# Attention results turned by transposes, two heads at a time, in halves of one PSUM bank

## The chip, the cores and the metric

The kernel runs on one core of a Trainium2 chip. The metric is the device time of one execution in microseconds; smaller is better. The engines are named as in the profile: PE (TensorE, matrix products), DVE (VectorE), ACT (ScalarE), POOL (GpSimd), and SP, which issues the DMAs.

## What is computed

Two layers over 2048 positions of width 1024. Each layer normalises x, projects it once, and gives the columns to four head groups of 256 columns each: A stick-breaking attention, B latent attention, C attention over the 256 best keys of each query, D differential attention. All results are gated, joined and projected back.

```python
def softmax_attention(q, k, v, scale):             # group B; C is the same over selected keys
    vis = chunk_visible(i, kk.shape[1])            # blocks of 128 queries, all keys up to the block
    s = einsum('bqhd,bshd->bhqs', qb, kk) * scale
    p = softmax(where(vis, s, -inf), axis=-1)
    return einsum('bhqs,bshd->bqhd', p, vv)

def diff_attention(...):                           # group D
    w = probs(q1b, k1b) - lam * probs(q2b, k2b)
    return einsum('bhqs,bshd->bqhd', w, vv)
y_d = rms_norm(od, diff_subln_g) * (1.0 - lam_init)
y = concatenate([silu(a_g) * y_a, silu(b_g) * y_b, silu(c_g) * y_c, silu(d_g) * y_d])
return x + einsum('bsn,nd->bsd', y, w_out)
```

## The kernel before

A layer is seven sweeps over 16 tiles of 128 queries, in the order a, h, d0, d1, b, c, o: group A with the scores of C's index, projections for later sweeps, the two halves of D, then B, C, and the output projection. For each tile of d0, d1, b and c there are units (two in d, four in b, two or four in c). A unit has a first part, which makes rows of probabilities (`att_row`: scores in PSUM, minimum and scaling on DVE, exponential with the sum on ACT, L847), and a second part, which multiplies them by the values (`att_pv`). The parts of neighbouring units, and projections of later tiles, are woven into each other by `merge` after costs that each part yields; the framework then orders the instructions of every engine by a timeline of its own, and each engine runs them in that order.

In `att_pv` the probabilities of up to four blocks of 128 keys are transposed on PE into a PSUM tile `tp` (L282), copied to SBUF by ACT (L284) or DVE (L286), and multiplied by the values (L866). The sums stand transposed in the PSUM tile `y`: even key blocks in partitions 0 to 63, odd ones in 64 to 127, and 128 columns for each head. `tp` has two buffers, `y` one, each a bank of 512 columns. In c and b one `y` holds four heads, in d two.

`att_out` finishes a tile. ACT copies `y` to SBUF (L875), and for each head PE multiplies that copy by `both`, two identity matrices of 64 above each other (L878). This adds even and odd blocks and turns the result, 128 queries by 64 columns. The product goes into `y` again. For b and c `norm_out` divides by the sums with one DVE product out of PSUM (L888) and writes 256 columns to `y` in DRAM (L889). In d two squares on ACT (L1093), the power -1/2 on POOL (`rstd`, L270 and L271), a small DVE product (L1095) and two larger ones (L1097) follow.

`y` serves other steps as well (`TG`): the transposes of queries and keys and the result of group A in sweep a (L354, L419, L431), and those of `prep_h` in sweep h (L1156). `o2` is the pool for what leaves, with two buffers. `psum` and `transposes` are helpers, so that most transposes have the line L282. The results wait in DRAM until sweep o reads them (L1302).

Of the kernel before, what the change touches and what calls it, by code (L numbers as in the profile page):

```python
# [10 lines left out]
F32 = mybir.dt.float32  # L11
# [29 lines left out]
EV = (0.6, 1.0, 0.6)  # L41
# [10 lines left out]
TG = {"ax": "pj", "at": "y", "ay": "y", "cp": "pj", "ct": "pj", "ao": "y", "kt": "pj", "dt": "pj", "ht": "y", "bt": "pj", "ot": "pj"}  # L52
# [55 lines left out]
class Trunk:  # L108
    def __init__(self, ctx, tc, I, out, layers=2):
        self.tc, self.nc, self.I, self.out, self.layers = tc, tc.nc, I, out, layers  # L110
        nc = self.nc
# [17 lines left out]
        ct = self.cst.tile  # L129
        ld = nc.sync.dma_start  # L130
# [3 lines left out]
        nc.scalar.copy(self.identr, self.ident)  # L134
        self.both = ct([128, 64], F32, name="both")
        ld(self.both, I["c_both"])
        self.identb = ct([128, 128], BF, name="identb")
# [20 lines left out]
        nc.vector.memset(self.chkC, float(TOPK))  # L158
        self.ev = 0


# [8 lines left out]
    def o2(self, shape, dtype=F32):  # L170

        return self.wk.tile(shape, dtype, name="o2", bufs=2)

# [5 lines left out]

    def psum(self, tag, shape=(128, 512)):  # L180
        return self.ps.tile(list(shape), F32, name=tag, bufs=PS[tag])

# [91 lines left out]
    def transposes(self, dst, srcs, eng="act", tag="pj"):  # L274

        nc = self.nc
        p = self.psum(tag, (128, 4, 128))
        m = srcs[0].shape[1]

        ident = self.identr if dst.dtype == F32R else self.ident  # L280
        for j, s in enumerate(srcs):
            nc.tensor.transpose(p[:m, j, :].bitcast(dst.dtype), s.bitcast(dst.dtype), ident)  # L282
        if eng == "act":
            nc.scalar.copy(dst, p[:m, :len(srcs), :])  # L284
        else:
            nc.vector.tensor_copy(dst, p[:m, :len(srcs), :])  # L286
# [402 lines left out]
    def ga_att(self, l, i, st):  # L689

        nc = self.nc
        yield 100.0
        t, v = st.pop(("a", i))
        o = i % 4 * 128
        nc.vector.tensor_copy(self.piece(st, "k", i, [128, 2, 512])[:, :, o:o + 128], t[:, 2:4])
        nc.vector.tensor_copy(self.piece(st, "v", i, [128, 4, 256])[:, i % 4, :], v)
        acc = self.o2([128, 2, 256])
        y = [self.psum("s", (128, 128)) for _ in range(2)]
        for b in range(i, -1, -1):
# [3 lines left out]
            for r in range(2):  # L703
# [3 lines left out]
                for p in range(2):  # L707
                    nc.tensor.matmul(z[r][:, p * 128:(p + 1) * 128], st["k"][b // 4][q, p, b % 4 * 128:b % 4 * 128 + 128], t[q, p, :],
                                     start=(b < i and p == 0), stop=True, skip_group_check=True)
# [14 lines left out]
            for p in range(2):  # L724
                for r in range(2):
                    hd = 2 * p + r
# [3 lines left out]
        ys = self.g2([128, 2, 128])  # L730
        for p in range(2):
            nc.vector.tensor_copy(ys[:, p], y[p])
        yo = self.g2([128, 2, 128])
# [135 lines left out]

    def att_out(self, i, y, nu):  # L870

        nc = self.nc
        h = 128 if i else 64
        ys = self.o2([128, 4, 128])
        nc.scalar.copy(ys[:h, :nu], y[:h].rearrange("p (a b) -> p a b", a=nu))  # L875
        p = self.psum(TG["ao"], (128, 4, 64))
        for u in range(nu):
            nc.tensor.matmul(p[:, u, :], ys[:h, u, :], self.both[:h], start=True, stop=True)  # L878
        return p[:, :nu]

    def norm_out(self, i, y, ls, col):

        nc = self.nc
        p = self.att_out(i, y, 4)
        rl = self.wk.tile([128, 4], F32, name="at_rl")
        nc.vector.reciprocal(rl, ls)
        yo = self.o2([128, 4, 64])
        nc.vector.tensor_mul(yo, p, rl[:, :, None].to_broadcast([128, 4, 64]))  # L888
        nc.sync.dma_start(self.y[i][:, col:col + 256].rearrange("p (a b) -> p a b", a=4), yo)  # L889

# [45 lines left out]
    def units_c(self, l, i, st):  # L936
        nb = i + 1
        ctx = {}
        m = 2 if i < PAIRED else 1
# [14 lines left out]
        def second(u):  # L954
            yield nb * m * 234.0 + 220.0
            if u == 0:
                ctx["y"] = self.psum("y")
            yield from self.att_pv(i, ctx[u], lambda j: st["cv"][j // 4][:, j % 4, :],
                                   ctx["y"][:, u * m * 128:(u + 1) * m * 128], EV[0])
            if u == 4 // m - 1:  # L960
                self.norm_out(i, ctx["y"], ctx["ls"], 512)
        return [(first(u), second(u)) for u in range(4 // m)]
# [82 lines left out]
    def units_d(self, l, i, st):  # L1045
# [32 lines left out]
        def second(u):  # L1078
# [6 lines left out]
            if u == 0:  # L1085
                return
            p = self.att_out(i, y[:, :256], 2)
            rl = wk.tile([128, 4], F32, name="at_rl")[:, :2]
            nc.vector.reciprocal(rl, ctx["l1"])
            yo = self.o2([128, 2, 64])  # L1090
            ss = wk.tile([128, 16], F32, name="ss")[:, :2]
            for h in range(2):
                nc.scalar.activation(yo[:, h], p[:, h], AF.Square, scale=rl[:, h:h + 1], accum_out=ss[:, h:h + 1])  # L1093
            rs = self.rstd("e", ss, 2, 64)
            nc.vector.tensor_mul(rs, rs, rl)  # L1095
            for h in range(2):
# [167 lines left out]
    def units_b(self, l, i, st):  # L1264
# [16 lines left out]
        def second(hd):  # L1281
            yield nb * 234.0 + 110.0
            if hd == 0:
                ctx["y"] = self.psum("y")
            yield from self.att_pv(i, [ctx[hd]], lambda j: st["bv"][j // 4][:, j % 4, hd * 64:(hd + 1) * 64],
                                   ctx["y"][:, hd * 128:(hd + 1) * 128], EV[2])
            if hd == 3:
                self.norm_out(i, ctx["y"], ctx["ls"], 256)
        return [(first(h), second(h)) for h in range(4)]
# [134 lines left out]
def consts():  # L1424
    import ml_dtypes
    r = np.arange(128)
    c = {}
    c["c_ident"] = np.eye(128, dtype=np.float32)
    c["c_both"] = np.tile(np.eye(64, dtype=np.float32), (2, 1))
    c["c_identb"] = np.eye(128, dtype=ml_dtypes.bfloat16)  # L1430
# [28 lines left out]
```

## Time and profile before

| | us |
|---|---|
| runs shown, median of 3 | 4232.53 (4230.74 to 4235.87) |
| profiled execution | 4232.69 |
| its span, first to last instruction | 4230.8 |
| mean granted clock of TensorE | 0.957 |

Busy time is the time in which an engine had an instruction at work. PE's instructions overlap, so a group's busy time is less than its count times its mean duration. A wait is the idle time of an engine before an instruction, put down to what released it.

### The profile page before, as it was taken

The page shows a single profiled execution, that of the slowest core. Times are in us where ns is not written, and L with a number is a line of the kernel's source. Part 1 is how long each engine was busy: PE and PEld are TensorE (multiplying, and loading weights), DVE is VectorE, ACT ScalarE, POOL GpSimd, SP SyncE. Part 2 cuts the span into 40 slices and gives each one's busy share as a digit, 9 for nine tenths or more (in the row PEclk, how much of TensorE's full clock was granted, in tenths as well). Part 3 has the DMA queues.
Part 4 walks back from the last instruction along what each step waited for, and adds up shares of the span by engine and source line. Part 5 has one row for each costly group of instructions (what it writes and reads, how often), then busy time and mean ns, then how long its engine had stood idle before and what let it go on. Part 6 is the DMA issues. An engine that isn't in the chain of part 4 may idle for free. (4 is left out here: it accounts for less than half of the span.)

```text
span 4230.8 us, 75339 instructions
## 1 busy us (share of the span) xinstructions
PE 3925.9 (93%) x25833; PEld 3246.6 (77%) x25833; DVE 2789.1 (66%) x10270; ACT 2318.9 (55%) x4790; POOL 1363.8 (32%) x2206
## 2 busy tenths in 40 slices
PE   6999997899988999999989999979899899999999
PEld 6887786778857777777878888768788577777787
DVE  3788677886876665563327897687868666555622
ACT  3566667565665554553125667666656555454621
POOL 2333212454554433210033332135444533232100
PEclk9999997999989999999999999979999799999999
DMA  3223552232210013214532236533232000132244
GB/s 125 100 94 124 180 183 86 83 85 89 86 37 26 18 38 100 79 46 142 164 109 102 100 117 212 159 94 93 77 96 82 27 20 19 48 102 69 68 134 138
DMA packets 227881, 396.49 MB, mean 94 GB/s; under 512 B 66336, under 2 KB 150432, under 8 KB 226976
## 3 DMA queue, kind: packets, MB, share of 16 engines
q1 hardware_dynamic: 227488, 391.59, 29.3%
q8 instruction: 206, 3.38, 0.3%
q14 instruction: 187, 1.53, 0.1%
HBM read 279.00 MB, written 112.49 MB: 93 GB/s over the span
## 5 line engine op out<-in xcount | busy, mean ns | idle before, releaser
L255 PE MATMUL pj<-w_hi,h_hi 128*128 128x384 f32 (+4 forms) x2560 | 872.6, 349 | 67.4 <-POOL w_hi L193 27.4
L256 PE MATMUL pj<-w_lo,h_hi 128*128 128x384 f32 (+4 forms) x2560 | 860.8, 344 | 9.9 <-POOL w_lo L187 6.3
L847 ACT ACTIVATE rw<-rw,at_mn 128x896 f32<-128x896 f32 (+15 forms) x512 | 615.8, 1204 | 171.6 <-DVE at_mn L846 151.6
L284 ACT COPY pt<-tp 128x512 f32<-128x512 f32 (+3 forms) x689 | 357.5, 529 | 431.3 <-PE tp L282 378.9
L255 PEld LDWEIGHTS pj<-w_hi,h_hi 128*128 128x128 f32 x2560 | 501.2, 196 | 104.8 <-POOL w_hi L193 31.0
L282 PE MATMUL tp<-ident,rw 128*128 128x128 f32 x3264 | 546.8, 289 | 36.6 <-DVE rw L1074 15.3
L259 PE MATMUL pj<-w_hi,h_lo 128*128 128x384 f32 (+4 forms) x2560 | 535.9, 339 | 0.0
L256 PEld LDWEIGHTS pj<-w_lo,h_hi 128*128 128x128 f32 x2560 | 501.2, 196 | 35.7 <-POOL w_lo L187 9.1
L282 PEld LDWEIGHTS tp<-ident,rw 128*128 128x128 f32 x3264 | 371.4, 145 | 174.0 <-issue 114.3
L843 DVE TENSOR_SCALAR_CACHE_REDUCE rw<-s 128x512 f32<-128x512 f32 x576 | 382.9, 685 | 125.2 <-PE s L837 80.2
L259 PEld LDWEIGHTS pj<-w_hi,h_lo 128*128 128x128 f32 x2560 | 439.2, 191 | 27.3 <-issue 11.5
L270 POOL TENSOR_SCALAR rs<-ss 128x2 f32<-128x2 f32 (+4 forms) x224 | 49.9, 223 | 1074.7 <-DVE ss L911 250.5
L538 ACT ACTIVATE junk<-sg,st_T 128x1152 int8<-128x1152 f32 (+4 forms) x224 | 293.8, 1311 | 75.3 <-DVE st_T L622 56.6
L271 POOL TENSOR_TENSOR rs<-rs,mhalf 128x8 f32<-128x8 f32 (+5 forms) x256 | 309.6, 1210 | 18.6
L286 DVE COPY pt<-tp 128x512 f32<-128x512 f32 (+3 forms) x247 | 153.2, 620 | 204.1 <-PE tp L282 164.9
L837 PE MATMUL s<-dk,qa 96*128 96x512 f32 (+3 forms) x640 | 235.0, 420 | 31.5 <-DVE rw L843 18.0
L837 PE MATMUL s<-bk,qa 128*128 128x512 f32 (+6 forms) x960 | 256.0, 391 | 2.2 <-DVE at_mn L841 1.6
L193 POOL TENSOR_SCALAR hl<-g 128x256 fp32r<-128x256 f32 (+1 forms) x384 | 143.8, 389 | 314.8 <-DVE g L452 60.1
L841 DVE CUSTOM_DVE_ANT_0 rw<-s,maskR 128x128 f32<-128x128 f32 (+3 forms) x400 | 187.7, 479 | 71.1 <-PE s L837 69.0
L187 POOL TENSOR_TENSOR hl<-g,hl 128x128 fp32r<-128x128 f32 (+1 forms) x384 | 215.7, 577 | 0.3
L866 PE MATMUL y<-pt,dv 128*64 128x128 f32 x2176 | 194.4, 305 | 19.8 <-DVE o L1097 12.4
L282 PE MATMUL pj<-identr,hl 128*128 128x128 f32 (+1 forms) x1280 | 172.9, 257 | 42.5 <-POOL hl L187 23.9
(267 smaller groups left out, 8256.2 us busy)
## 6 DMA issues: line engine op xcount, KB each, us to landing
h_hi<-hT SPq DMA_DIRECT2D x128, 512.0 KB, 3.8
h_lo<-hT SPq DMA_DIRECT2D x128, 512.0 KB, 4.9
x4a<-x SPq DMA_DIRECT2D x32, 512.0 KB, 4.8
hT<-h_hi SPq DMA_DIRECT2D x32, 512.0 KB, 2.7
hT<-h_lo SPq DMA_DIRECT2D x32, 512.0 KB, 3.4
x4a<-y SPq DMA_DIRECT2D x32, 512.0 KB, 3.5
x4b<-gate SPq DMA_DIRECT2D x32, 512.0 KB, 3.7
x4c<-x SPq DMA_DIRECT2D x32, 512.0 KB, 4.2
```

The source lines that it names most:

```text
L187: self.nc.gpsimd.tensor_sub(o, a, b)
L255: nc.tensor.matmul(p[:, :n], hi[:, k, :], whi[k], start=(k == 0), stop=False)
L256: nc.tensor.matmul(p[:, :n], hi[:, k, :], wlo[k], start=False, stop=False)
L259: nc.tensor.matmul(p[:, :n], lo[:, k, :], whi[k], start=False, stop=(k == kt - 1))
L271: nc.gpsimd.tensor_tensor(r, r, self.mhalf[:, :n], op=OP.pow)
L282: nc.tensor.transpose(p[:m, j, :].bitcast(dst.dtype), s.bitcast(dst.dtype), ident)
L284: nc.scalar.copy(dst, p[:m, :len(srcs), :])
L538: nc.scalar.activation(self.junk[:, :ns[g]], Sg[g], AF.Sign, bias=th[:, g:g + 1], scale=-1.0, accum_out=dst[:, g:g + 1])
L837: nc.tensor.matmul(p[:, :w], x, y, start=(k == 0), stop=(k == len(ops) - 1))
L843: nc.vector.tensor_scalar(o, p[:, :w], -scale, None, op0=OP.mult, op1=OP.min, accum_out=m)
L847: nc.scalar.activation(rw, rw, AF.Exp, bias=mn, scale=-1.0, accum_out=ls)
L866: nc.tensor.matmul(y[o:o + 64, :], v(j), pt[:, c * m:(c + 1) * m, :].rearrange("p a b -> p (a b)"), start=(j < 2), stop=(j >= nb - 2), ski ...
```

## The change

`y` becomes one tile that is made once, `halves`, two times 256 columns of one bank, and each call for `y` takes the other half. Transposes into `y` are done two at a time. `att_out` always takes two heads: ACT copies their sums to SBUF, PE transposes each head's block (128 by 128) into a buffer of `tp`, ACT copies both to SBUF, and POOL adds the columns of even and odd key blocks. `norm_out` is called for each pair of heads; its product by the reciprocal sums moves from DVE to POOL, and it writes 128 columns. In d the small product of `rs` and `rl` moves to POOL, and the squares and the last products read SBUF. `both` is gone, `o2` has four buffers, and an accumulator of the general path `ga_att`, which the profiled execution doesn't enter, takes its tile from another pool.

```diff
@@ -132,8 +132,6 @@
         ld(self.ident, I["c_ident"])
         self.identr = ct([128, 128], F32R, name="identr")
         nc.scalar.copy(self.identr, self.ident)
-        self.both = ct([128, 64], F32, name="both")
-        ld(self.both, I["c_both"])
         self.identb = ct([128, 128], BF, name="identb")
         ld(self.identb, I["c_identb"])
         self.maskA = ct([128, 256], BF, name="maskA")
@@ -157,6 +155,8 @@
         self.chkC = ct([128, layers, NT], F32, name="chkC")
         nc.vector.memset(self.chkC, float(TOPK))
         self.ev = 0
+        self.halves = self.ps.tile([128, 2, 256], F32, name="y", bufs=1)
+        self.nhalf = 0
 
 
     def g2(self, shape, dtype=F32):
@@ -169,7 +169,7 @@
 
     def o2(self, shape, dtype=F32):
 
-        return self.wk.tile(shape, dtype, name="o2", bufs=2)
+        return self.wk.tile(shape, dtype, name="o2", bufs=4)
 
     def x4(self, which, shape, dtype=F32):
         return self.wk.tile(shape, dtype, name="x4" + which, bufs=1)
@@ -178,6 +178,11 @@
         return self.wk.tile([128, 6, 128], F32R, name="qa", bufs=QA)
 
     def psum(self, tag, shape=(128, 512)):
+        if tag == "y":
+
+            self.nhalf ^= 1
+            y = self.halves[:, self.nhalf]
+            return y if len(shape) == 2 else y.rearrange("p (a b) -> p a b", b=shape[-1])
         return self.ps.tile(list(shape), F32, name=tag, bufs=PS[tag])
 
     def padd(self, o, a, b):
@@ -274,7 +279,11 @@
     def transposes(self, dst, srcs, eng="act", tag="pj"):
 
         nc = self.nc
-        p = self.psum(tag, (128, 4, 128))
+        if tag == "y" and len(srcs) > 2:
+            for j in range(0, len(srcs), 2):
+                self.transposes(dst[:, j:min(j + 2, len(srcs))], srcs[j:j + 2], eng, tag)
+            return
+        p = self.psum(tag, (128, 2 if tag == "y" else 4, 128))
         m = srcs[0].shape[1]
 
         ident = self.identr if dst.dtype == F32R else self.ident
@@ -867,26 +876,32 @@
                                  start=(j < 2), stop=(j >= nb - 2), skip_group_check=True)
             yield (109.0 + 125.0) * m * len(js)
 
-    def att_out(self, i, y, nu):
+    def att_out(self, i, y):
 
         nc = self.nc
         h = 128 if i else 64
-        ys = self.o2([128, 4, 128])
-        nc.scalar.copy(ys[:h, :nu], y[:h].rearrange("p (a b) -> p a b", a=nu))
-        p = self.psum(TG["ao"], (128, 4, 64))
-        for u in range(nu):
-            nc.tensor.matmul(p[:, u, :], ys[:h, u, :], self.both[:h], start=True, stop=True)
-        return p[:, :nu]
+        ys = self.o2([128, 2, 128])
+        nc.scalar.copy(ys[:h], y[:h].rearrange("p (a b) -> p a b", a=2))
+        p = self.psum("tp", (128, 4, 128))
+        for u in range(2):
+            nc.tensor.transpose(p[:, u, :h], ys[:h, u, :], self.ident[:h, :h])
+        po = self.o2([128, 2, 128])
+        nc.scalar.copy(po[:, :, :h], p[:, :2, :h])
+        if i == 0:
+            return po[:, :, :64]
+        yo = self.o2([128, 2, 64])
+        self.padd(yo, po[:, :, :64], po[:, :, 64:])
+        return yo
 
     def norm_out(self, i, y, ls, col):
 
         nc = self.nc
-        p = self.att_out(i, y, 4)
-        rl = self.wk.tile([128, 4], F32, name="at_rl")
+        rl = self.wk.tile([128, 2], F32, name="at_rl", bufs=4)
         nc.vector.reciprocal(rl, ls)
-        yo = self.o2([128, 4, 64])
-        nc.vector.tensor_mul(yo, p, rl[:, :, None].to_broadcast([128, 4, 64]))
-        nc.sync.dma_start(self.y[i][:, col:col + 256].rearrange("p (a b) -> p a b", a=4), yo)
+        p = self.att_out(i, y)
+        yo = self.o2([128, 2, 64])
+        self.pmul(yo, p, rl[:, :, None].to_broadcast([128, 2, 64]))
+        nc.sync.dma_start(self.y[i][:, col:col + 128].rearrange("p (a b) -> p a b", a=2), yo)
 
 
     def start_c(self, l, st):
@@ -953,12 +968,15 @@
 
         def second(u):
             yield nb * m * 234.0 + 220.0
-            if u == 0:
+            h = u * m
+            if h % 2 == 0:
                 ctx["y"] = self.psum("y")
+            o = h % 2 * 128
             yield from self.att_pv(i, ctx[u], lambda j: st["cv"][j // 4][:, j % 4, :],
-                                   ctx["y"][:, u * m * 128:(u + 1) * m * 128], EV[0])
-            if u == 4 // m - 1:
-                self.norm_out(i, ctx["y"], ctx["ls"], 512)
+                                   ctx["y"][:, o:o + m * 128], EV[0])
+            h += m
+            if h % 2 == 0:
+                self.norm_out(i, ctx["y"], ctx["ls"][:, h - 2:h], 512 + (h - 2) * 64)
         return [(first(u), second(u)) for u in range(4 // m)]
 
 
@@ -1084,15 +1102,15 @@
                                    y[:, u * 128:(u + 1) * 128], EV[1])
             if u == 0:
                 return
-            p = self.att_out(i, y[:, :256], 2)
-            rl = wk.tile([128, 4], F32, name="at_rl")[:, :2]
+            rl = wk.tile([128, 2], F32, name="at_rl", bufs=4)
             nc.vector.reciprocal(rl, ctx["l1"])
+            p = self.att_out(i, y)
             yo = self.o2([128, 2, 64])
             ss = wk.tile([128, 16], F32, name="ss")[:, :2]
             for h in range(2):
                 nc.scalar.activation(yo[:, h], p[:, h], AF.Square, scale=rl[:, h:h + 1], accum_out=ss[:, h:h + 1])
             rs = self.rstd("e", ss, 2, 64)
-            nc.vector.tensor_mul(rs, rs, rl)
+            self.pmul(rs, rs, rl)
             for h in range(2):
                 nc.vector.scalar_tensor_tensor(yo[:, h], p[:, h], rs[:, h:h + 1], gsub, op0=OP.mult, op1=OP.mult)
             o = 768 + 128 * st["half"]
@@ -1280,12 +1298,13 @@
 
         def second(hd):
             yield nb * 234.0 + 110.0
-            if hd == 0:
+            if hd % 2 == 0:
                 ctx["y"] = self.psum("y")
+            o = hd % 2 * 128
             yield from self.att_pv(i, [ctx[hd]], lambda j: st["bv"][j // 4][:, j % 4, hd * 64:(hd + 1) * 64],
-                                   ctx["y"][:, hd * 128:(hd + 1) * 128], EV[2])
-            if hd == 3:
-                self.norm_out(i, ctx["y"], ctx["ls"], 256)
+                                   ctx["y"][:, o:o + 128], EV[2])
+            if hd % 2 == 1:
+                self.norm_out(i, ctx["y"], ctx["ls"][:, hd - 1:hd + 1], 256 + (hd - 1) * 64)
         return [(first(h), second(h)) for h in range(4)]
```

## Rows read from the trace of the kernel before

**Rows 1.** The page's first part: busy time by engine

```profile
PE 3925.9 (93%) x25833; PEld 3246.6 (77%) x25833; DVE 2789.1 (66%) x10270; ACT 2318.9 (55%) x4790; POOL 1363.8 (32%) x2206
```

**Rows 2.** Stretches: us, busy us (x count) by engine, PEclk, DMA share, GB/s

```profile
0.00:436.00 436.00, 381.82 (x2361) 332.49 (x2362) 318.36 (x1163) 243.12 (x526) 141.01 (x195) 0.98 0.33 110
...
660.00:1268.00 608.00, 541.14 (x3876) 463.40 (x3875) 473.10 (x1784) 376.53 (x822) 284.34 (x466) 0.91 0.26 77
1268.00:1637.00 369.00, 353.59 (x2745) 281.16 (x2745) 224.66 (x774) 198.22 (x410) 135.33 (x250) 0.98 0.12 34
1637.00:1957.00 320.00, 310.21 (x2178) 233.97 (x2176) 178.07 (x563) 165.64 (x287) 72.78 (x116) 0.99 0.24 75
1957.00:2130.00 173.00, 171.26 (x795) 137.56 (x795) 57.20 (x89) 33.20 (x58) 8.51 (x10) 1.00 0.55 181
```

**Rows 3.** PE's groups: busy us, mean ns | idle before, releasers

```profile
L282 PE MATMUL tp<-ident,rw 128*128 128x128 f32 x3264 | 546.8, 289 | 36.6 <-DVE rw L1074 15.3 <-ACT pt L284 10.8 <-DVE pt L286 3.5
...
L878 PE MATMUL y<-both,o 128*128 128x64 f32 (+1 forms) x768 | 106.1, 275 | 1.2 <-ACT o L875 1.0
```

**Rows 4.** A hand-off in sweep c, in order of time: start, us

```profile
3873.84 1.09 PE L282 MATMUL tp<-ident,rw 128*128 128x128 f32 x8
...
3874.89 1.10 PE L878 MATMUL y<-both,o 128*128 128x64 f32 x8
...
3875.83 1.05 PE L282 MATMUL tp<-ident,rw 128*128 128x128 f32 x8
...
3876.03 0.42 DVE L888 TENSOR_TENSOR o<-y,at_rl 128x256 f32<-128x256 f32 x1 [0.35 <-PE y L878]
...
3876.81 1.52 PE L866 MATMUL y<-pt,cv 128*64 128x256 f32 x12
```

**Rows 5.** What PE waited for: us in total, times, longest us

```profile
PE pj L282 <- POOL hl L187: 23.9, 19, 3.2
...
PE y L866 <- DVE o L1097: 16.9, 9, 4.8
...
PE tp L282 <- ACT pt L284: 10.8, 13, 3.6
...
PE y L878 <- ACT o L875: 1.0, 3, 0.5
```

**Rows 6.** The end of one tile of sweep d, in order of time

```profile
2998.01 0.37 ACT L875 COPY o<-y 128x256 f32<-128x256 f32 x1 [0.83 <-PE y L866]
...
2998.44 0.66 PE L878 MATMUL y<-both,o 128*128 128x64 f32 x4
...
3003.74 0.19 POOL L270 TENSOR_SCALAR rs<-ss 128x2 f32<-128x2 f32 x1
...
3006.73 0.47 DVE L1097 SCALAR_TENSOR_TENSOR o<-y,rs,gsub 128x64 f32<-128x64 f32 x2
```

**Rows 7.** ACT's groups, shapes kept apart

```profile
L875 ACT COPY o<-y 128x512 f32<-128x512 f32 x60 | 35.2, 586 | 38.0 <-PE y L866 37.8
...
L875 ACT COPY o<-y 128x256 f32<-128x256 f32 x60 | 22.1, 368 | 36.8 <-PE y L866 36.5
...
L284 ACT COPY qa<-y 128x512 f32<-128x512 f32 x32 | 18.8, 588 | 5.3 <-PE y L282 5.3
```

**Rows 8.** GpSimd's groups, shapes kept apart

```profile
L190 POOL TENSOR_TENSOR tab<-ci_cs,gain 128x128 f32<-128x128 f32 x64 | 31.5, 512 | 2.7 <-DMA ci_cs<-c_rope 2.0 <-DVE g L1042 0.6
...
L184 POOL TENSOR_TENSOR rw<-rw 128x128 f32<-128x128 f32 x40 | 21.2, 530 | 2.9
...
L187 POOL TENSOR_TENSOR qb<-g,qb 128x32 fp32r<-128x32 f32 x32 | 8.6, 268 | 0.0
```

**Rows 9.** DVE's groups, shapes kept apart

```profile
L1074 DVE SCALAR_TENSOR_TENSOR rw<-rw,d_c 128x512 f32<-128x512 f32 x192 | 163.8, 890 | 2.1
...
L1311 DVE TENSOR_TENSOR x4a<-x4a,x4b 128x512 f32<-128x512 f32 x64 | 41.5, 686 | 33.1 <-DMA x4a<-y 15.6 <-ACT x4b L1307 11.7 <-ACT h_hi L1315 5.8
```

More of the change, by code (lines that the diff above doesn't have):

```diff
@@ L696, in ga_att @@
         nc.vector.tensor_copy(self.piece(st, "v", i, [128, 4, 256])[:, i % 4, :], v)
-        acc = self.o2([128, 2, 256])
+        acc = self.pt([128, 2, 256])
         y = [self.psum("s", (128, 128)) for _ in range(2)]
@@ L1428, in consts @@
     c["c_ident"] = np.eye(128, dtype=np.float32)
-    c["c_both"] = np.tile(np.eye(64, dtype=np.float32), (2, 1))
     c["c_identb"] = np.eye(128, dtype=ml_dtypes.bfloat16)
```

## The prediction

> **What bounds the kernel now.** I read the page's first part, then a table of busy time by stretch, then PE's groups and waits, and last two places in the order of time. TensorE (PE) is busy for 3925.9 of 4230.8 us, and GpSimd (POOL) for a third [rows 1]. The stretches show that this is not one limit: sweep b (1268 to 1637 us) and sweep c (1637 to 1957) have PE busy for 354 of 369 and 310 of 320 us at a granted clock of 0.98 and 0.99, so that there PE's work is the time. Sweeps d0 and d1 (660 to 1268) have PE busy for 541 of 608 at 0.91, with DVE at 473: a mixture of PE's work and of waits on DVE, POOL and ACT [rows 2]. The second layer repeats these sweeps.
>
> **PE's work.** For each head, `att_out` multiplies the saved result by `both` (L878): 4 heads in 64 calls (b, c) and 2 heads in 64 calls (d) make 384 products, in the trace 768 instructions, 106.1 us of busy time [rows 3]. The change puts 384 transposes of a 128x128 float32 block in their place. That operation is in the trace: the transposes of probabilities (L282 into `tp`) are one instruction each, 3264 for 546.8 us, or 0.168 us each [rows 3]. So 384 x 0.168 = 64.3 us stand for 106.1, a saving of 41.8 us. The order of time says the same: eight L878 start at 3874.89 and what follows them at 3875.83, 0.94 us for four heads; eight transposes start at 3873.84 and L878 follows at 3874.89, 1.05 us, or 0.52 for four [rows 4]. 0.94 - 0.52 = 0.42 for four heads, times 96 such sets, is 40 us.
>
> By count 256 of the 384 are in b and c, where PE is the limit: 27.9 us, counted in full. The other 128 are in d: 13.9 us, counted at PE's busy share there, 541/608, so 12.4. Together -40.3. Fewer instructions also mean fewer weight loads, and I give nothing for that.
>
> **The hold of `y`.** Before, `y` is one PSUM buffer which serves the sums, and then the product of L878; it comes free only when the last reader of that product is done. In d that is a long way round: copy by ACT at 2998.01, L878 at 2998.44, squares on ACT, the power on POOL (its first step at 3003.74), L1097 ending at 3007.20. That is 9.2 us [rows 6]. PE stood for it 9 times, 16.9 us in all [rows 5]. After it, the copy alone (0.37 us, [rows 6]) ends the hold, since the product goes into `tp` and is copied on to SBUF. What is late next at these places is the following unit's own probabilities, so I take half: -8; bounds 0 and -16.9.
>
> In b and c `y` now changes hands after two heads, 128 times instead of 64, and GpSimd's share comes behind. PE's list of waits has no entry for L888, the reader which released `y` there [rows 5]: at the one shown, `y` is free at 3876.45 and PE is in transposes until 3876.81 [rows 4]. The new hand-off needs ACT's copy only. The next sums must in any case wait for their own first transposes and these for an eviction, so I put it at 0. If that cover is gone the price is the copy, 0.37 us each; that is the slow rival below.
>
> **`tp`.** The two transposes take one of two slots until ACT has copied them out, so the next unit's second set of transposes waits for copy, transposes and copy. An ordinary eviction has the same length, and waits for evictions by ACT cost PE 10.8 us over all sweeps [rows 5]. The transposes themselves stand at the head of PE's queue until the copy of `y` is done: L878 paid 1.0 us in 128 calls for this [rows 5], 192 calls pay 1.5.
>
> **ACT.** 192 copies of 256 columns at 0.368 replace the copies of 512 (35.2 us) and 256 (22.1) [rows 7], and 192 more at the same price bring the transposes to SBUF: 141 for some 61 (the few small ones included), +80. In sweeps a and h each set of transposes into `y` becomes two (2+2 and 2+1), which costs ACT 2 x 0.37 - 0.59 = 0.15 for each of the 32 in a [rows 7] and about as much in h, +10 in all. ACT goes from 55% to 57%. What waits behind a copy are exponentials and evictions; bounds 0 to 192 x 0.37 = 71 if PE stood for each second copy. I take +4 with the 1.5 above in it, near the bottom, because so little of PE's waiting is for ACT now.
>
> In a and h the second pair may have to wait until the first is copied, if the two halves are kept apart as one bank: 64 x 0.37 = 24 at most, 0 where other work covers it, and -1 or so if the halves run freely. Sweep a has PE busy for 382 of 436 us [rows 2], which leaves other causes of idle time as cover: +4.
>
> **GpSimd and DVE.** Added on POOL are 192 additions and 128 products of 128 elements, for which the nearest rows give 0.51 and 0.53 us, and 64 products of 2 elements at 0.27 or less [rows 8]: 320 x 0.52 + 64 x 0.27 = 184 us, 32% to 37%. These results are needed sweeps later, or by a late step of d, so they do not hold PE. But the splits of projections queue behind them on POOL, and PE waits for those: 23.9 us for L187 [rows 5]. The load of POOL in d and b rises by a tenth to a quarter, so between 0 and as much again; I take +6. DVE loses L888 and L1095, some 40 us less the extra reciprocals, mostly off PE's path: 0. The y transfers in b and c double in number and halve in size; they wait on SP for POOL instead of DVE, and loads behind them may start later. I put that inside the +6.
>
> There is a reason in the trace against moving work to POOL. L1074, which reads two SBUF tensors, takes 890 ns for 512 columns in sweep d, where POOL is 47% busy; L1311, also with two SBUF inputs of that width, takes 686 in sweep o, where POOL is 5% busy [rows 2, 9]. The difference of 0.2 us on 192 instructions is 39 us of DVE; POOL's added tenth in d would add 4, and I leave it in the range. The Trainium skill, page "GPSIMD Engine Reference", section "Key points", names this: GpSimd shares its SBUF interfaces with VectorE and contends with DVE instructions that have two SBUF inputs. The two rows agree with it, though the operations differ.
>
> **Sum.** -40.3 - 8 + 4 + 4 + 6 = -34.3. The profiled execution took 4232.7 (span 4230.8 and 1.9 around it), 0.2 over the median, so 4198 on the median's scale. With ACT's bound of 71 left to the slow rival, the bounds of the other terms run from -41.8 - 16.9 = -58.7 (4174) to -40.3 + 4 + 24 + 24 = +11.7 (4244).
>
> **Rivals.** *Each hand-off is exposed (slower).* The halves lie in one bank. If a write into one half is ordered after the read of the other, alternating buys no overlap, and PE stands for ACT's copy each time. Price: 128 hand-offs in b and c and 64 in a and h, 192 x 0.37 = 71 us, so 4198 + 71 - 4 = 4265. It decides from 34/192 = 0.18 us exposed for each. Against it: b and c keep PE fed at 96% through hand-offs of 1.5 us (3874.89 to 3876.45) [rows 2, 4]. For it: they come twice as often. The Trainium skill, page "PSUM — Partial Sum Buffer", section "PSUM bank collisions raise a hardware error", says that guards should go by bank and quadrant, not by address; that is this rival's condition, and no row of before shows two halves in use. Chance 0.18.
>
> *The relief is spent elsewhere (same).* d ends on DVE, and PE's saving in d and at `y` turns into waits for L1074 and its like, while POOL's queue and the copies take as much as b and c give: 27.9 against 24 (POOL's whole bound) gives 4228. It needs POOL's waits to double. Chance 0.17.
>
> *More comes back (faster).* d's clock of 0.91 between the two levels 1.2 and 2.4 GHz means 18% of 608 us at the lower, 219 us over both layers. If the 16.9 us of waits go wholly, and with them an eighth of d's 134 us of PE idle time, and low stretches shrink in proportion, 27 us at half speed return 14. Together -41.8 - 16.9 - 14 + 14 = -59, or 4174; with POOL's and ACT's costs at nothing 4160. Chance 0.13.
>
> **Numbers.** The forecast holds 0.52, most of it within 25 us of its value. Faster by over 0.2% (8.5 us, about what a measurement tells from no change): 0.52 and 0.13, and a little of the same case, 0.67; same 0.15; slower 0.18. The range goes from 4160 to 4250, which leaves out half of the slow rival and the tails.
>
> **What would show it.** In the profile after: no L878, 384 more transposes into `tp` at 0.17 us of busy time; PE's busy time down by 40; the wait of `y` for DVE gone in d; waits of `y` for ACT below 0.18 us per hand-off; POOL up by 184 us, ACT by 90; b and c shorter by some 13 us in each layer, d by 10. I am wrong if b and c do not get shorter, or if PE's idle time grows by more than 35 us.

## The result

The changed kernel takes 4299.56 us (median of 5, 4297.81 to 4304.52), beside 4232.58 of the kernel before: ratio 1.0153 (95% interval 1.014 to 1.0167), 67 us slower. The forecast was 4198. The profiled execution took 4304.5, its span is 4302.7 us, 71.9 longer, at nearly the same mean clock (0.956); it is the slowest of the five.

PE's busy time was to fall by 40 us. The page of the changed kernel shows it risen by 25.9 instead, and the span by more than that, so PE's idle time rose too, from 304.9 to 350.9 us. ACT rose by 77 and GpSimd by 153:

```profile
PE 3951.8 (92%) x25449; PEld 3200.4 (74%) x25449; DVE 2768.1 (64%) x10206; ACT 2395.9 (56%) x5108; POOL 1517.0 (35%) x2578
```

Line numbers have moved: the products with the values, L866 before, are L875 now; ACT's copy of `y`, L875 before, is L884, and the new copy of the transposed result L889; the evictions of `tp` (its copies to SBUF), L284 and L286, are L293 and L295. Four words are used below. A *hand-off* is the passing of `y` from the sums of one pair of heads (before, of one tile) to the next. The *block* is the two transposes that turn a pair of heads (in the kernel before, the products by `both` in their place), a *set* the up to four transposes that share a buffer of `tp`, and a *run* of products a row of them with no other PE instruction between.

PE's groups of the changed kernel (busy us, mean ns | idle before) have two lines to set against [rows 3]. The block's transposes (L887; a smaller form for the first tiles brings them to 384 and 78.2 us) are 27.9 us cheaper than the 768 products. The same 3264 transposes of probabilities (now L291) cost 15.1 us more than before:

```profile
L291 PE MATMUL tp<-ident,rw 128*128 128x128 f32 x3264 | 561.9, 291 | 49.6 <-DVE rw L1092 25.0 <-ACT o L889 9.8 <-POOL rw L189 5.5
...
L887 PE MATMUL tp<-ident,o 128*128 128x128 f32 x360 | 73.4, 286 | 12.1 <-ACT o L884 11.5
```

PE's waits in the changed kernel (us in total, times, longest), against [rows 5]: the 16.9 us for L1097 are gone, the head of the block's transposes waits 20.6 us for ACT's copy of `y` where L878 waited 1.0, and the products wait 40.3 us (24.4 and 15.9) for evictions of `tp`:

```profile
PE pj L291 <- POOL hl L192: 34.1, 29, 7.8
...
PE y L875 <- ACT pt L293: 24.4, 38, 2.5
PE tp L887 <- ACT o L884: 20.6, 27, 4.5
...
PE y L875 <- DVE pt L295: 15.9, 25, 1.4
...
PE tp L291 <- ACT o L889: 9.8, 11, 3.4
```

Before, the products' wait for evictions was 15.4 us:

```profile
PE y L866 <- DVE pt L286: 8.5, 13, 1.4
...
PE y L866 <- ACT pt L284: 6.9, 9, 2.8
```

So the wait at the block itself grew by 19.6 us, and the products' wait for evictions by 24.9.

Where in the kernel: the lengths of the sweeps, each counted from the start of the last result's DMA of one sweep to that of the next, both layers added (us; the last two columns are experiments described below).

| sweep | before | after | e1_y_half | e13_y_whole |
|---|---|---|---|---|
| a | 935.8 | 953.7 | 950.5 | 940.8 |
| h | 302.1 | 308.4 | 310.3 | 301.0 |
| d0 and d1 | 1262.8 | 1254.9 | 1246.9 | 1259.0 |
| b | 731.2 | 759.8 | 730.4 | 729.7 |
| c | 671.5 | 710.8 | 638.9 | 637.5 |
| o | 317.4 | 306.4 | 315.2 | 317.5 |

Sweeps b and c, where the prediction counted its surest gain, are 68 us longer, nearly the whole loss; the others change by -11 to +18 and together by 5. The four stretches b, c, b, c of the changed kernel (us, then PE, PEld, DVE, ACT and POOL busy, clock, DMA share, GB/s) show PE idle for 25.5, 23.0, 25.6 and 15.2 us; before, cut in the same way, it was 14.3, 10.2, 11.6 and 8.4. Of the 68 us, 45 are idle time of PE and 23 are busy time. The clock stays at 0.96 to 0.99, near the upper of its two levels:

```profile
1261.60:1639.80 378.20, 352.68 (x2658) 274.83 (x2658) 218.69 (x781) 207.29 (x456) 163.71 (x310) 0.97 0.12 35
1639.80:1994.50 354.70, 331.65 (x2166) 236.10 (x2167) 176.86 (x556) 178.17 (x333) 102.45 (x177) 0.97 0.23 72
3412.90:3794.50 381.60, 355.99 (x2663) 276.90 (x2661) 219.11 (x781) 211.06 (x461) 164.82 (x316) 0.96 0.12 35
3794.50:4150.60 356.10, 340.86 (x2247) 246.45 (x2248) 177.64 (x563) 182.69 (x337) 95.02 (x167) 0.99 0.25 78
```

PE's instructions in the order of time show what has changed. One hand-off in sweep c of the changed kernel (start, us, count, idle before):

```profile
3955.49 0.65 PE L875 MATMUL y<-pt,cv 128*64 128x256 f32 x4
3956.07 0.72 PE L846 MATMUL s<-ck,qa 128*128 128x512 f32 x2
3956.63 0.51 PE L264 MATMUL pj<-w_hi,h_lo 128*128 128x384 f32 x2
3956.98 0.38 PE L887 MATMUL tp<-ident,o 128*128 128x128 f32 x2
3957.20 0.60 PE L291 MATMUL tp<-ident,rw 128*128 128x128 f32 x4
3958.05 0.66 PE L291 MATMUL tp<-ident,rw 128*128 128x128 f32 x4 [0.25 <-ACT o L889]
3958.63 0.65 PE L875 MATMUL y<-pt,cv 128*64 128x256 f32 x4
3959.22 0.66 PE L291 MATMUL tp<-ident,rw 128*128 128x128 f32 x4
3960.04 0.65 PE L875 MATMUL y<-pt,cv 128*64 128x256 f32 x4 [0.17 <-DVE pt L295]
3960.62 0.66 PE L291 MATMUL tp<-ident,rw 128*128 128x128 f32 x4
```

Before, eight transposes of the next unit ran ahead of L878 and more behind it, and the products then came twelve at a time [rows 4]. Here no transpose of the next unit stands between the last products (3955.49) and the block (3956.98); scores and a piece of a projection fill the time there. The next unit begins behind the block, its second set waits for the copy of the block (0.25 us), and PE then goes to and fro, four transposes and four products. That no transpose stands ahead of the block is so throughout. By the starts of PE's instructions, the mean number of transposes of probabilities between a pair's last product and its block was 4.2 in b and 5.3 in c before; after the change it is 0 in every one of the 192 hand-offs.

A part of the rise of PE's busy time comes with it. The profile models where a PE instruction ends, so these are times from a start to the next start, idle time left out. A product that another product follows takes 0.067 us on the mean and the last of a run 0.23; a transpose of probabilities that another follows takes 0.13, the last ahead of a product 0.22 to 0.23. The kernel before has 700 runs of products, the changed one 810, and `e1_y_half` below 697; the changed kernel has 122 more such last transposes than `e1_y_half`. By these means that is 113 x 0.16 + 122 x 0.10, some 30 us more for the same work, about half of the 63.5 us by which the busy times of the two differ. The other half was not traced to a cause.

### The profile page after: what moved, and what is told of

It reads as the page before. It is cut to its first block, busy times and chain, and to the rows that moved or that the text cites. A ratio compares the mean times of both kernels' runs of the same rounds, so it can differ in the third digit from the quotient of the medians.

```text
span 4302.7 us, 75444 instructions
## 1 busy us (share of the span) xinstructions
PE 3951.8 (92%) x25449; PEld 3200.4 (74%) x25449; DVE 2768.1 (64%) x10206; ACT 2395.9 (56%) x5108; POOL 1517.0 (35%) x2578
## 4 chain that ended last, share of the span: by engine, by line
PE 60%; DVE 17%; ACT 8%; POOL 5%; issue 5%; DMA 5%; SPq 0%; ACTq 0%; POOLq 0%; DVEq 0%
PE y L875 9%; PE s L846 8%; PE pj L260 8%; PE tp L291 8%; PE pj L261 7%; PE pj L264 7%; PE s L260 3%; PE s L261 3%; PE s L264 3%; DVE sc L515 2%; ACT junk L547 2%; DMA w_raw<-w_in 2%; PE pj L291 2%; ACT rw L856 2%; DVE rw L850 1%
## 5 line engine op out<-in xcount | busy, mean ns | idle before, releaser
L260 PE MATMUL pj<-w_hi,h_hi 128*128 128x384 f32 (+4 forms) x2560 | 877.5, 351 | 70.9 <-POOL w_hi L198 25.9
L291 PE MATMUL tp<-ident,rw 128*128 128x128 f32 x3264 | 561.9, 291 | 49.6 <-DVE rw L1092 25.0
L293 ACT COPY pt<-tp 128x512 f32<-128x512 f32 (+3 forms) x689 | 359.4, 529 | 408.5 <-PE tp L291 390.8
L264 PE MATMUL pj<-w_hi,h_lo 128*128 128x384 f32 (+4 forms) x2560 | 524.1, 339 | 0.0
L291 PEld LDWEIGHTS tp<-ident,rw 128*128 128x128 f32 x3264 | 373.2, 145 | 188.4 <-issue 116.7
L295 DVE COPY pt<-tp 128x512 f32<-128x512 f32 (+3 forms) x247 | 153.1, 620 | 272.6 <-PE tp L291 255.3
L189 POOL TENSOR_TENSOR o<-o 128x128 f32<-128x128 f32 x180 | 89.9, 499 | 508.7 <-ACT o L889 457.6
L291 PE MATMUL pj<-identr,hl 128*128 128x128 f32 (+1 forms) x1280 | 174.7, 258 | 51.6 <-POOL hl L192 34.1
L514 ACT ACTIVATE pt<-s 128x512 f32<-128x512 f32 (+3 forms) x304 | 158.3, 547 | 109.0 <-DVE sc L515 60.7
```

The source lines that it names most:

```text
L260: nc.tensor.matmul(p[:, :n], hi[:, k, :], whi[k], start=(k == 0), stop=False)
L264: nc.tensor.matmul(p[:, :n], lo[:, k, :], whi[k], start=False, stop=(k == kt - 1))
```

## The experiments

Times are medians; a ratio is to the kernel before on the same chip, with its 95% interval.

| run | us | ratio |
|---|---|---|
| e1_y_half | 4205.34 | 0.9932 (0.991 to 0.9953) |
| e7_before_tp | 4279.09 | 1.0121 (1.01 to 1.0142) |
| e2_dve | 4294.55 | 1.014 (1.0123 to 1.0157) |
| e3_whole | 4294.45 | 1.0134 (1.0117 to 1.0151) |
| e5_both | 4225.76 | 0.9985 (0.9974 to 0.9997) |
| e4_four | 4202.51 | 0.9931 (0.9911 to 0.995) |
| e6_defer | 4303.82 | 1.0172 (1.0153 to 1.0191) |
| e10_split | 4266.10 | 1.01 (1.008 to 1.012) |
| e12_dummy_y | 4231.16 | 1.001 (0.9999 to 1.002) |
| e11_dummy_tp | 4285.60 | 1.0135 (1.0115 to 1.0155) |
| e14_dummy_free | 4209.58 | 0.9951 (0.9935 to 0.9968) |
| e15_dummy_late | 4250.49 | 1.0045 (1.0028 to 1.0062) |
| e9_y_dve | 4222.90 | 0.9975 (0.9963 to 0.9987) |
| e13_y_whole | 4194.63 | 0.9922 (0.9902 to 0.9942) |

**The block's place.** The changed kernel with one line other:

```diff
-        p = self.psum("tp", (128, 4, 128))
+        p = self.psum("y", (128, 2, 128))
         for u in range(2):
             nc.tensor.transpose(p[:, u, :h], ys[:h, u, :], self.ident[:h, :h])
```

> The changed kernel (4299.6 us) with one edit: the two transposes of att_out go into the other half of y instead of a buffer of tp. Theory tp (the result's block takes one of the two tp buffers for a round trip over ACT, so the next unit's transposes of probabilities can't run ahead): most of the loss comes back, 4200 to 4245 us, and ACT's and POOL's added work stays. Theory ACT (two copies per pair stand in ACT's queue in front of evictions and exponentials): unchanged, 4285 to 4315. Theory POOL and theory splits (a, h): unchanged as well.

The place alone is worth 94 us, and without it the change is a gain. PE's page line and a hand-off of this kernel in sweep c:

```profile
PE 3888.3 (93%) x25449; PEld 3203.2 (76%) x25449; DVE 2769.0 (66%) x10206; ACT 2391.1 (57%) x5110; POOL 1516.7 (36%) x2578
...
3850.80 1.08 PE L875 MATMUL y<-pt,cv 128*64 128x256 f32 x8
3851.82 0.76 PE L291 MATMUL tp<-ident,rw 128*128 128x128 f32 x5
3852.42 0.44 PE L887 MATMUL y<-ident,o 128*128 128x128 f32 x2
3852.91 0.66 PE L291 MATMUL tp<-ident,rw 128*128 128x128 f32 x4
3853.49 1.08 PE L875 MATMUL y<-pt,cv 128*64 128x256 f32 x8
3854.51 0.66 PE L291 MATMUL tp<-ident,rw 128*128 128x128 f32 x4
```

Five transposes stand ahead of the block again (4.6 on the mean in b, 5.3 in c), and the next products are eight in a row: 1.02 us from start to start, where the changed kernel takes 0.59 for four. PE's busy time is 63.5 us below the changed kernel's for the same instructions, with 697 runs of products.

The reverse, on the kernel before: its product by `both` goes into `tp`.

```diff
-  "ao": "y"
+  "ao": "tp"
```

> The kernel before (4232.6 us) with one edit: the product by both goes into a buffer of tp instead of y. Both theories of tp: slower, by the 95 us that the block's place made in the changed kernel for 192 blocks, times 128/192, so 4275 to 4310; in the trace no transpose of probabilities stands between the last sums and L878. Theory that the loss needs the second ACT copy as well (here DVE frees the block at once): 4232 to 4250.

47 us for 128 blocks, with no transposed block, no second copy, no halves and no new work on GpSimd: 0.37 us each, against 0.49 for the 192 above. Here too no transpose stands between last product and block, in all 128.

**GpSimd, and the splits of sweeps a and h.** The change with additions and products back on DVE:

```diff
-        self.padd(yo, po[:, :, :64], po[:, :, 64:])
+        nc.vector.tensor_add(yo, po[:, :, :64], po[:, :, 64:])
...
-        self.pmul(yo, p, rl...)
+        nc.vector.tensor_mul(yo, p, rl...)
```

> The changed kernel with the additions and both products on DVE instead of POOL. Theory POOL (splits of projections queue behind the new work and PE waits for them): 4230 to 4260. Theories tp and ACT: within 12 us of the changed kernel, 4288 to 4312, as DVE has a third of its time free.

The change with the transposes of three and four in a and h whole:

```diff
-            for j in range(0, len(srcs), 2):
-                self.transposes(dst[:, j:min(j + 2, len(srcs))], srcs[j:j + 2], eng, tag)
-            return
+            p = self.halves.rearrange("p a (b c) -> p (a b) c", c=128)
...
```

> The changed kernel, but sets of three and four transposes in sweeps a and h go into the whole bank at once, with one copy, as before the change. Theory splits (the second pair waits for the first pair's copy): sweeps a and h return to 611 and 614 us per layer from 635 and 627, 4260 to 4275 in all. Theories tp, ACT and POOL: within 12 us of the changed kernel.

Each gives back 5 us of 67, and its interval overlaps that of the change; neither is the cause. In `e3_whole` sweeps a and h are as short as before (1238.6 us together, 1237.9 before, 1262.1 after the change; the kernel before has 630 and 608 by layer in this cut, not the expectation's 611 and 614), but later sweeps give most of that back.

**Halves and hand-offs of two heads alone.** The change, but with the product by `both` into the other half and DVE reading it there:

```diff
-        p = self.psum("tp", (128, 4, 128))
-            nc.tensor.transpose(p[:, u, :h], ys[:h, u, :], self.ident[:h, :h])
+        p = self.psum("y", (128, 2, 128))
+            nc.tensor.matmul(p[:, u, :64], ys[:h, u, :], self.both[:h], start=True, stop=True)
...
+        return p[:, :, :64]
```

> Halves and hand-offs of two heads as in the changed kernel, but the result is turned by the product with both into the other half of y, and DVE takes it from PSUM; no second ACT copy, no block in tp, no POOL work. It isolates the halves and the doubled hand-offs with PE's old work. Theory tp: 4225 to 4250. Theory ACT: half of the loss stays, 4255 to 4280, since 192 copies of y instead of 128 remain. Theory hand-off (twice as many turns of y in b and c by themselves): 4280 or more.

At 0.9985 nothing is lost by twice as many hand-offs and the split sets of a and h together. PE's saving without the halves is measured on the kernel before with the transposes of all its heads in `y`, one copy by ACT, and the rest on GpSimd:

```diff
-        p = self.psum(TG["ao"], (128, 4, 64))
-            nc.tensor.matmul(p[:, u, :], ys[:h, u, :], self.both[:h], start=True, stop=True)
+        p = self.psum("y", (128, 4, 128))
+            nc.tensor.transpose(p[:, u, :h], ys[:h, u, :], self.ident[:h, :h])
+        po = self.o2([128, 4, 128])
+        nc.scalar.copy(po[:, :nu, :h], p[:, :nu, :h])
...
```

> The kernel before with the transposes alone: four heads (two in d) in the whole bank of y, one ACT copy out of it, addition and product on POOL; no halves, no block in tp. PE's cheaper work by itself, 4232.6 - 40 and some 6 back for POOL and ACT: 4190 to 4210. If the halves are what pays in the variant with the block in y (4205), this stays at 4220 or above, since y is held for one more ACT copy.

It gives 29 us, as much as `e1_y_half` (0.9931 and 0.9932): the halves add nothing that can be told. It is not PE's cheaper work alone, since DVE's product goes to GpSimd here too, and `e9_y_dve` below shows that this counts.

**Why the place costs.** First the block was written later, behind the next unit's first two sets of transposes, together with the copy of `y`:

```diff
             if self.ev >= 1:
                 self.ev -= 1
+            if j0 == step or nb <= step:
+                self.flush()          # att_out and what follows of the unit before
...
```

> The changed kernel with its block still in tp, but att_out of a pair is written behind the next unit's first two sets of transposes (first one, where a unit has one). Two theories of why the block in tp costs so much. Order: buffers of tp are given out in the order of the program, so no transpose of the next unit can pass the block, and PE has nothing between the last sums and the block; then the later place brings most back, 4205 to 4240 us. Occupancy: one of two buffers is gone for ACT's round trip wherever it is taken; then 4275 or more.

No gain, and not conclusive, since the copy of `y`, for which the block waits, went back with it: `tp` waited 44.3 us for that copy. So the copy stayed in its place and the block alone was moved:

```diff
+                y = self.att_save(i, ctx["y"])          # the copy to SBUF, at once
-                self.norm_out(i, ctx["y"], ...)
+                self.late = lambda: self.norm_out(i, y, ...)
```

> The change with the block in tp as it is, but written later: the copy of y to SBUF stays where it was, and the two transposes of the block, their copy and what follows are written behind the next unit's first two sets of transposes. Theory order (the buffers of tp are handed out in the written order, and the block holds back the next unit's transposes because it has to wait for the last product and the copy of y): by the time the block's turn comes its copy is long done, so most of the 94 us that the block's place cost comes back, 4205 to 4240 us. Rival occupancy (the block costs because it takes one of two buffers from first transpose to the end of ACT's copy, some 0.8 to 1 us, whenever it comes): 4270 to 4305, as the change. Between: both have a share.

It gives back 22 of the 94 us (1.0100 against 1.0153). Theory order wanted most of it back, and as stated it fails here; 4266 lies just below the rival's range, where the expectation gives both a share. To part the wait from the hold, one transpose that nobody reads was added to `e1_y_half`. It goes into `tp`, or as a control into `y`:

```diff
+        t = self.psum("tp", (128, 4, 128))                                # e11
+        nc.tensor.transpose(t[:, 0, :h], ys[:h, 0, :], self.ident[:h, :h])
...
+        nc.tensor.transpose(p[:, 0, :h], ys[:h, 0, :], self.ident[:h, :h])  # e12, p is in y
```

> The variant with the block in the other half of y (4205 us), and beside it one transpose of the copied y into a buffer of tp that nobody reads: it takes a buffer for one transpose, 0.15 us, and needs no copy by ACT, but it stands in the written order between the units. Work added on PE: 192 transposes of 0.168, at most 32 us. Theory order: the next unit's transposes can't pass it, so the time is well above its control (the same transpose into y): control plus 50 us or more, 4270 to 4310. Rival occupancy: a buffer held for 0.15 us costs little, control plus 0 to 15.

> The control of the dummy in tp: the same added transpose of the copied y, but into the half of y that the block's own transposes overwrite at once. Both theories: the added work alone, 0 to 32 us above 4205, so 4205 to 4238.

The same transpose costs 54 us more in `tp` than in `y`, though no copy holds its buffer. In `e11_dummy_tp` no transpose of probabilities stands between last product and block in any of the 192, and there are 809 runs of products; in `e12_dummy_y` they are 4.8 (b) and 5.4 (c), with 706 runs. The control itself is 33 us (0.0078) above `e1_y_half`, the full price of its 192 transposes. Then the wait was taken away with the taker left in its place (the transpose is of a constant), and the taker moved behind the next unit's two sets:

```diff
-        nc.tensor.transpose(t[:, 0, :h], ys[:h, 0, :], self.ident[:h, :h])
+        nc.tensor.transpose(t[:, 0, :h], self.ident[:h, :], self.ident[:h, :h])   # e14
...
+            ys, h = self.late                                   # e15, in flush, as in e6
+            nc.tensor.transpose(t[:, 0, :h], ys[:h, 0, :], self.ident[:h, :h])
```

> The variant with the block in the other half of y, and one transpose into a buffer of tp that nobody reads, at the same place in the written order, but of a constant (the identity), so that it has no copy to wait for. Its two relatives: the same transpose of the copied y into y took 1.001 of before, into tp 1.0135. Theory wait (the next unit's transposes stand behind a taker of tp that has to wait for the last product and ACT's copy of y): without that wait the time is near the first, 1.000 to 1.004 of before, 4226 to 4245. Rival turn (a third taker in the order of the two buffers costs by itself, since it ties each set of transposes to the one before it): near the second, 1.010 to 1.015, 4270 to 4295.

> The variant with the block in the other half of y, and the unread transpose of the copied y into tp, written behind the next unit's first two sets of transposes. Theory wait: the copy is done by then and nobody reads the buffer, so near the control, 1.000 to 1.005 of before, 4226 to 4250; what the deferred block itself still lost (1.010) is then ACT's copy out of tp, for which a buffer stays taken. Rival turn: a taker of tp at any place costs, 1.008 to 1.014, 4262 to 4290.

Without the wait the extra taker costs nothing that can be told from `e1_y_half` (0.9951 against 0.9932, intervals overlapping), although it is 192 more transposes for PE, and 5.5 (b) and 6.0 (c) transposes pass ahead of the block. That is below both ranges of the expectation, on the side of theory wait. Moved behind two sets it costs 15 us over the control (1.0045 against 1.0010), inside the range of theory wait. The added transposes in PE's groups, of `e11_dummy_tp` and then of `e14_dummy_free`, show the difference in what they wait for:

```profile
L887 PE MATMUL tp<-ident,o 128*128 128x128 f32 x180 | 52.9, 294 | 12.7 <-ACT o L884 12.1
```

```profile
L887 PE MATMUL tp<-ident 128*128 128x128 f32 x180 | 58.0, 322 | 3.2 <-ACT pt L293 2.4 <-DVE pt L295 0.3
```

So the wait is shown: a taker of `tp` that waits for the last product and for ACT's copy of `y` keeps back every later transpose into `tp`. It is worth 54 us against the control in `y`, and 78 us (0.0184) against `e14_dummy_free`. The rest of the 94, 40 or 16 us by subtraction, was not parted by a run of its own. Three things point to the hold, the buffer being taken until ACT has copied the block: the little that `e10_split` gives back, `e15_dummy_late`, whose late taker is not copied and which is 23 us (0.0055) faster than `e10_split`, and the 0.25 us in the hand-off above. But when a block is written elsewhere the whole order of PE changes with it (`e10_split` has 881 runs of products, the change 810), so the size of the hold stays open.

**GpSimd again, and a better version.** With the block in `y`, additions and products on DVE, as in `e2_dve`:

> The block in the other half of y (4205) and additions and products on DVE instead of POOL. On top of the changed kernel the move to DVE gave 5 us; if it adds up, 4195 to 4204. If DVE is nearer to PE's path once tp no longer is, 4205 to 4220.

Slower by 0.0043 of the time, 18 us, than `e1_y_half` with them on GpSimd, and the intervals don't touch: with the block in `y`, GpSimd is the better place for them. On DVE the change keeps a gain of 0.0025, 11 us, over the kernel before. And with the block in `y` and the transposes of a and h whole, as in `e3_whole`:

> The variant with the block in the other half of y, and the transposes of three and four in sweeps a and h whole, into both halves at once, as before the change. With tp in the way this edit was worth 5 us, while sweeps a1 and h0 alone were shorter by 22 and 8; if what they gained was lost behind them to the block in tp, it now shows: 4185 to 4200. If sweeps a and h only move work between them and what follows, 4200 to 4208.

At 0.9922 it is the fastest median of the study, 31 us below the kernel before on its chip. Against `e1_y_half` and `e4_four` the intervals overlap.

## Why the prediction was wrong

**The step that failed** is the paragraph on `tp`. It saw that "the two transposes take one of two slots until ACT has copied them out" and priced this at nothing but 1.5 us at the head of PE's queue, because "an ordinary eviction has the same length". The place is worth 94 us (4299.56 against 4205.34), 0.49 us for each of 192 blocks. An ordinary set of transposes needs rows that an earlier first part has made. The block's cannot begin before the unit's last product and ACT's copy of it (0.37 us), and the sets behind it use the same two buffers in turn. Before, L878 had these same waits but wrote into `y`, so the next unit's transposes could be placed ahead of it: the eight at 3873.84 in [rows 4] are just that. They were in the rows, and the prediction read them as a price of transposes and not as the cover that hides the copy. Moving the block to `tp` took away this cover, 192 times. For `y` the prediction had asked the right question ("If that cover is gone the price is the copy"); it did not ask it for `tp`.

**PE's work** came as forecast but was covered up. The 384 transposes have 78.2 us of busy time, not 64.3: two in a row take 0.38 to 0.44 us, where the price was a mean over sets of four and eight. Counted from start to start, block work fell by 37.6 us in the whole trace (84.6 to 47.0), beside the -40.3 of the sum. With the block in `y` sweeps b and c together are 33.4 us shorter (forecast 27.9), sweep d 15.9 (forecast 12.4 and 8). The split within b and c was not as forecast: b is as long as before, since PE's busy time there falls by 14.3 us and its idle time rises by 13.5, and c has the whole gain.

**The hold of `y`**: the wait for L1097 is gone, as said, and sweep d is 7.9 us shorter; at `y` itself no wait of the products for ACT's copy L884 came up in the changed kernel. Putting the hand-offs in b and c at nothing was right for the halves alone (`e5_both`).

**ACT**: +77 us busy, forecast +90. **GpSimd**: +153, forecast 184; its additions take 0.50 us as priced, its products 0.43 against 0.52. PE's wait for the splits of projections on it rose by 10.2 us [rows 5], forecast 6, but taking the work off GpSimd gave 5 us, within the intervals, or lost 18. **The split sets** in a and h lengthen these sweeps by 24.2 us, which is the upper bound given; at the end of the kernel they are worth 5 (`e3_whole`) or, with the block in `y`, 11 (`e13_y_whole`), both within overlapping intervals, beside the +4 taken.

**The rivals.** "Each hand-off is exposed" had the right sign at 4265, and not the mechanism: it put the stop at `y`, between the halves, and there it is not, as `e1_y_half` and `e5_both` use the halves as much and lose nothing. The stop is at the block's transposes, the head of PE's queue. 4300 lies beyond even that rival's price, which counted only the copy; waits of the products for evictions (+24.9 us) and more turns between transposes and products (some 30 us) came on top. The two signs named for being wrong both came true: b and c longer, PE's idle time up by 46 us.

Together, with the failed step taken out: 4205 measured where the sum gave 4198. That it is so near is in part luck: b, c and d give 49.3 us where 48.3 were counted, but a and h are 22.9 us longer in that run, where +4 was taken, and the +10 taken for ACT and GpSimd has no measurement of its own.

## What to carry to other kernels

Before a short-lived result is put into a small pool of buffers that a stream of other work uses in turn, ask what that result waits for. Where the buffers are given out in the written order, as here, the pool's later users wait with it, and all that ran in the shadow of its wait comes to light. In the trace, look at what stands between the producer and the result now; if it is work on the very buffers that the result is to use, that work is the cover which will be lost. A busy share near full doesn't say that only work counts: with a worse order PE's busy time was 63 us higher for the same instructions.

## What was not expected of the hardware

PE's turns between kinds of work have a price in these traces that stands in busy time and in no wait: from start to next start the last product of a run takes 0.23 us where one inside it takes 0.067, and eight products in a row take 1.02 us, where four take 0.59.

The two halves of one bank are not free of each other in this program. In `e1_y_half` the sums of the next pair go into the half that the block isn't in, and yet the profile puts 15.4 us of PE's idle time before the products down to ACT's read of the block (a row of its waits); each of the 15 products starts 0.05 us after the end of that copy:

```profile
PE y L875 <- ACT o L889: 15.4, 15, 3.4
```

The Trainium skill, page "PSUM — Partial Sum Buffer", section "PSUM bank collisions raise a hardware error", asks for guards by bank and quadrant; this wait agrees with it. It is an order that the program keeps by a semaphore; no run was made without it, so what the chip itself needs is not shown, nor what the wait costs in the end. It is also the condition of the rival "Each hand-off is exposed", at 15.4 us in place of 71.

DVE work moved to GpSimd paid with the block in `y`: `e1_y_half` is 18 us faster than `e9_y_dve`, though an addition of 128 columns takes 0.50 us on GpSimd and 0.33 on DVE. In `e9_y_dve` DVE was busy for 67% and GpSimd for 32%. Under the block in `tp` the same move shows no difference clear of noise (`e2_dve`). Why it paid was not tested.
